# Splitting the second layer's mixing weights ahead in steps of three pieces

## The chip, the cores and the metric

The kernel runs on one core of one Trainium2 chip. The metric is the device time of one execution in microseconds (us); the time before is the median of three runs. Engines are named as in the profile: PE (TensorE matmuls), PEld (TensorE weight loads), DVE (VectorE), ACT (ScalarE), POOL (GpSimd), SP (SyncE, here the engine whose queue issues the DMAs).

## The reference

Two layers over 512 latent and 256 context tokens of width 1024. Each layer has a mixing part (one input projection `w_in`, then a gated MLP group A, a differential attention group B and a convolution group C, then one output projection `w_out`) and a gated feed-forward part of inner width 2816. Only the latent stream is returned. Cut to what matters here:

```python
for l in range(DEPTH):
    hl = modulate(rms_norm(x_lat, norm1_g[l]), sh1, sc1)
    pa, q, k, v, pc = project(hl, P, rope)            # hl @ w_in[l]
    o = blocked_diff_attn(q, k_all, v_all, lam)
    x_lat = x_lat + g1 * mixer_merge(pa, o, pc, P, lam_init)   # [ya, yb, yc] @ w_out[l]
    h2 = modulate(rms_norm(x_lat, norm2_g[l]), sh2, sc2)
    x_lat = x_lat + g2 * conv_ffn(h2, P)
def conv_ffn(h, P):
    gt = dwconv(h @ P["w_gate"], P["ffn_conv_w"], P["ffn_conv_b"])
    return (jax.nn.silu(gt) * (h @ P["w_val"])) @ P["w_down"]
```

The context tokens go through the same layer 0; in layer 1 they only give keys and values.

## The kernel before, in words

**Products.** Every FP32 product is made of three: each operand is split into a rounded part `hi` and a rest `lo = x - hi`, and PE adds hi·hi, hi·lo and lo·hi (`mm3`, L266 to L268). So each weight tile must be split before PE can use it: it is loaded as `raw` (L216, 512 KB for 128x1024), cast to `whi` on ACT (L224), and `wlo = raw - whi` follows on DVE or, for some tiles, on POOL (`sub_lo`, L110). `raw` has three buffers, `whi` and `wlo` two each, so the next cast waits until PE has left the tile before the last one.

**Feed-forward.** It runs in two halves of 11 inner tiles. A gate tile takes two weight tiles of `w_gv` (products `pp`), then `ft` (convolution, SiLU, product) and the split of its result into `gh` (ACT, L1028) and `gl`. After 11 gate tiles come four down steps (`w_down`, products `pd`), each over two output columns of `xT`; the last step of half 1, the tail, does the context and the latent tokens in two blocks.

**Splitting ahead.** Layer 1's mixing weights are split during layer 0's feed-forward by `split_ahead` (L237 to L252), a generator that is made at the end of half 0. For each of 56 pieces (40 of `w_in`, 16 of `w_out`, 128x512 each) it loads `araw` (L247), casts `ahi` (ACT, L248), subtracts in place (DVE, L110) and stores both parts to DRAM (L250, L251). Three buffers of each are there. Layer 1 then loads the finished parts as `wh` and `wl` (`wsplit_of`, L261) with no split. The code asks for three pieces after a gate tile of half 1 and for eight after a down step (`AHEAD`), at a priority lowered by 60 (`ALOW`). A scheduler orders each engine's instructions by priority and readiness; on the chip an engine runs them strictly in that order. The trace has the pieces between 598 and 789 us, that is from half 0's down steps on.

SP's queue is in order too: a load that has to wait until its buffer's store has landed holds every later load.

Of the kernel before, what the change touches and what calls it, by code (L numbers as in the profile page):

```python
# [53 lines left out]

WE = "dpdpdpdddppdpppppddp"


AHEAD = (3, 8)

AH = ((4, 1), (18, 1))  # L60
KH = ((6, 10, 27, 31, 35, 39), (17, 17, 25, 34, 35, 48))
CH = ((41, 3), (40, 5))
N1H, N1P = 5, 2
ALOW = 60

VEV = 2

# [13 lines left out]
def tile_backbone(  # L81
# [24 lines left out]
    def low(n):  # L106
        return tc.high_priority(offset=-n)
# [127 lines left out]
        return w_in[l, 2 * k2 * P:(2 * k2 + 2) * P, col:col + 512].rearrange("(a p) n -> p a n", p=P)  # L235

    def split_ahead(sp):  # L237
        todo = [(("in", col, k2), [w_cols(1, col, k2)[:, a] for a in range(2)])
                for col in (COL_K, COL_C, COL_A, COL_Q, COL_V) for k2 in range(KD // 2)]
        todo += [(("out", q, mp2), [w_out[1, q, mp2, :, i].rearrange("p k m -> p (k m)") for i in range(2)])  # L240
                 for mp2 in range(KD // 2) for q in range(2)]
        for key, srcs in todo:
            split[key] = dram.tile([P, 2, 2, 512], F32, name="_".join(map(str, key)))
            for a, src in enumerate(srcs):
                raw = sp.tile([P, 512], F32, tag="araw", name="araw", bufs=3)
                hi = sp.tile([P, 512], F32R, tag="ahi", name="ahi", bufs=3)
                nc.sync.dma_start(out=raw, in_=src)  # L247
                S.copy(hi, raw)  # L248
                sub_lo(raw, raw, hi)
                nc.sync.dma_start(out=split[key][:, 0, a], in_=hi.bitcast(F32))  # L250
                nc.sync.dma_start(out=split[key][:, 1, a], in_=raw)  # L251
                yield  # L252

    def wsplit_of(key, src, shape, eng, tags=("hi", "lo"), p=None, **kw):
        if key not in split:
# [18 lines left out]
    class Norm:  # L274
# [6 lines left out]
        def add(self, k, g):  # L281
            a, b, _ = g
            if g not in self.begun:
                self.begun.add(g)
                S.activation(self.ss[:, a:b], xT[:, k, a:b], AF.Square)
            else:
                sq = self.p.tile([P, 512], F32, tag="nsq", name="nsq", bufs=self.nb)
                S.activation(sq[:, :b - a], xT[:, k, a:b], AF.Square)
                V.tensor_add(self.ss[:, a:b], self.ss[:, a:b], sq[:, :b - a])

        def rstd(self, g, ps, tag, bufs):
            a, b, _ = g
# [29 lines left out]
    for l in range(DEPTH):  # L322
# [636 lines left out]
        with ExitStack() as ph:  # L959
# [22 lines left out]
            for half in range(2):  # L982
                gh = hp.tile([P, HJ, toks], F32R, tag="gh", name="gh", bufs=1)
                gl = hp.tile([P, HJ, toks], F32R, tag="gl", name="gl", bufs=1)
                for jj in range(HJ):
                    j = half * HJ + jj
                    pp = [[ps.tile([P, 512], F32, tag="acc", name="pp", bufs=8) for g in range(2)]
                          for s in range(nseg)]
                    w = [wsplit(w_gv[l, j, g], [KD, P], "dve") for g in range(2)]

                    def gv(g, seg):
                        a, b, s = seg
                        o = pp[s][g][:, a - SEG[s][0]:b - SEG[s][0]]
                        for k in range(KD):
                            mm3(o, w[g][0][:, k], w[g][1][:, k], hhi[:, k, a:b], hlo[:, k, a:b], k == 0, k == KD - 1)

                    if j == 0:
                        for seg in ngs:
                            if seg == g1:
                                for k in range(KD):  # L1000
                                    r = norm2.apply(l, 1, g1, k, hhi, hlo)
                                tab["since"].append(r.ins)
                                table(T_SILU)
                            for g in range(2):
                                gv(g, seg)
                                if seg == g0 and g == 1:
                                    norm2.rstd(g1, ps, "acc", 8)
                    else:
                        for g in range(2):
                            for seg in whole:  # L1010
                                gv(g, seg)
                    if j == 0 and not last:
                        start_dots(norm2.last)
                    t = sp.tile([P, TOK], F32, tag="ft", name="ft", bufs=FTB)
                    for s in range(nseg):
                        a, b = SEG[s]
                        gp = pp[s][0]
                        n = b - a
                        S.activation(t[:, a:b], gp[:, :n], AF.Identity, bias=fb[:, l, j:j + 1], scale=fw[:, l, j, 1:2])
                        V.scalar_tensor_tensor(out=t[:, a + 1:b], in0=gp[:, 0:n - 1], scalar=fw[:, l, j, 0:1],  # L1020
                                               in1=t[:, a + 1:b], op0=ALU.mult, op1=ALU.add)
                        V.scalar_tensor_tensor(out=t[:, a:b - 1], in0=gp[:, 1:n], scalar=fw[:, l, j, 2:3],  # L1022
                                               in1=t[:, a:b - 1], op0=ALU.mult, op1=ALU.add)
                    act(t[:, :toks], t[:, :toks], AF.Silu)
                    for s in range(nseg):
                        a, b = SEG[s]
                        V.tensor_mul(t[:, a:b], t[:, a:b], pp[s][1][:, :b - a])  # L1027
                    S.copy(gh[:, jj], t[:, :toks])  # L1028
                    sub_lo(gl[:, jj], t[:, :toks], gh[:, jj])
                    if not last and half:  # L1030
                        with low(ALOW):
                            for _ in zip(range(AHEAD[0]), ahead):
                                pass
                chunks = [(j0, min(4, HJ - j0)) for j0 in range(0, HJ, 4)]
                for mp2 in range(KD // 2):
                    tail = half == 1 and mp2 == KD // 2 - 1
                    ws = {}
                    for gi, gs in enumerate([[g] for g in ngs] if tail else [whole]):
                        pd = {g: [ps.tile([P, 512], F32, tag="acc", name="pd", bufs=8) for i in range(2)] for g in gs}
                        cs_ = chunks[::-1] if gi else chunks  # L1040
                        for ci, (j0, jn) in enumerate(cs_):
                            if not (gi and ci < 2):
                                src = w_down[l, mp2, :, half * HJ + j0:half * HJ + j0 + jn]
                                ws[j0] = wsplit(src, [jn, 256], "dve", p=wt if tail and not last else None)
                            wh, wl = ws[j0]
                            for jj in range(jn):
                                if gi and not last and (ci, jj) == (0, N1P):
                                    next_norm(ngs[0], ps, "acc", 8)
                                st_, sp_ = ci == 0 and jj == 0, ci == len(cs_) - 1 and jj == jn - 1
                                for g in gs:  # L1050
                                    a, b, s = g
                                    for i in range(2):
                                        ms = slice(i * P, (i + 1) * P)
                                        mm3(pd[g][i][:, :b - a], wh[:, jj, ms], wl[:, jj, ms],
                                            gh[:, j0 + jj, a:b], gl[:, j0 + jj, a:b], st_, sp_)
                        if not last and half:
                            with low(ALOW):
                                for _ in zip(range(AHEAD[1]), ahead):
                                    pass
                        for g in gs:  # L1060
                            a, b, s = g
                            for i in range(2):
                                m = 2 * mp2 + i
                                V.scalar_tensor_tensor(out=xT[:, m, a:b], in0=pd[g][i][:, :b - a],
                                                       scalar=modv[:, l, s, 5, m:m + 1],
                                                       in1=xT[:, m, a:b], op0=ALU.mult, op1=ALU.add)
                                if half == 1:
                                    if last:
                                        nc.sync.dma_start(out=out[:, m, a:b], in_=xT[:, m, a:b])
                                    else:  # L1070
                                        norm.add(m, g)
                        if tail and not last:
                            if gi == 0:
                                table(T_LNEXP)
                                hhi, hlo = [hb.tile([P, KD, TOK], F32R, tag=t, name=t) for t in ("hhi", "hlo")]
                if not last and half == 0:
                    dots.close()
                    cstack.close()
                    wt = pool(ph, "wt", "left")
                    ahead = split_ahead(wt)  # L1080
        pss_.close()
    hbs.close()
    nstack.close()
# [84 lines left out]
```

## Time and profile before

| what | us |
|---|---|
| median of three runs | 1620.43 (1617.92 to 1620.6) |
| profiled execution | 1616.07 |
| its span | 1614.0 |
| PE busy | 1570.6 (97%) |
| DVE busy | 1020.4 (63%) |
| ACT busy | 646.9 (40%) |
| POOL busy | 105.9 (7%) |

The profile comes from one execution, 4.4 us shorter than the median. PE is busy in nearly all of it, so time can be lost in two ways: PE idle, or PE at a lower granted clock (a column of its own, in shares of full speed). A wait is listed by engine, line, and what released it. Times at a row's start are us from the span's start; idle time before an instruction stands behind it in brackets.

### The profile page before, as it was taken

The page shows a single profiled execution, that of the slowest core. Times are in us where ns is not written, and L with a number is a line of the kernel's source. Part 1 is how long each engine was busy: PE and PEld are TensorE (multiplying, and loading weights), DVE is VectorE, ACT ScalarE, POOL GpSimd, SP SyncE. Part 2 cuts the span into 40 slices and gives each one's busy share as a digit, 9 for nine tenths or more (in the row PEclk, how much of TensorE's full clock was granted, in tenths as well). Part 3 has the DMA queues.
Part 4 walks back from the last instruction along what each step waited for, and adds up shares of the span by engine and source line. Part 5 has one row for each costly group of instructions (what it writes and reads, how often), then busy time and mean ns, then how long its engine had stood idle before and what let it go on. Part 6 is the DMA issues. An engine that isn't in the chain of part 4 may idle for free.

```text
span 1614.0 us, 21207 instructions
## 1 busy us (share of the span) xinstructions
PE 1570.6 (97%) x8186; PEld 1292.4 (80%) x8186; DVE 1020.4 (63%) x1722; ACT 646.9 (40%) x1122; POOL 105.9 (7%) x126
## 2 busy tenths in 40 slices
PE   6999998999999999999999999999999999999999
PEld 4875776778888887878888887887778788888888
DVE  4497878969999983345544244896976544334433
ACT  5431568753532322234433133254764333123321
POOL 1130125310000000000000000000220000000000
PEclk9999999999999999999999999999999999999999
DMA  7625110015255888988611235653022322332232
GB/s 282 212 76 180 56 64 15 14 51 185 85 190 194 285 279 265 289 284 298 207 66 50 60 127 186 205 170 105 27 80 78 104 92 88 95 104 92 92 105 92
DMA packets 83140, 222.93 MB, mean 138 GB/s; under 512 B 12256, under 2 KB 14560, under 8 KB 82912
## 3 DMA queue, kind: packets, MB, share of 16 engines
q1 hardware_dynamic: 83040, 221.59, 41.6%
q8 instruction: 64, 1.05, 0.3%
q14 instruction: 36, 0.29, 0.1%
HBM read 190.10 MB, written 31.46 MB: 137 GB/s over the span
## 4 chain that ended last, share of the span: by engine, by line
PE 77%; DMA 10%; DVE 6%; ACT 4%; issue 2%; SPq 0%; POOL 0%; POOLq 0%; DVEq 0%; ACTq 0%
PE pp L267 10%; PE pp L266 10%; PE pp L268 10%; PE acc L433 5%; PE acc L441 5%; PE acc L434 5%; PE pd L268 4%; PE pd L267 4%; PE pd L266 4%; DMA in<-araw 3%; DMA araw<-in_w_in_dram 3%; PE po L860 3%; PE wo L266 2%; DMA mraw<-in_w_modT_dram 2%; PE wo L267 2%; PE wo L268 2%
## 5 line engine op out<-in xcount | busy, mean ns | idle before, releaser
L268 PE MATMUL pp<-hhi,wlo 128*128 128x512 f32 (+1 forms) x1072 | 380.0, 355 | 4.4 <-DVE wlo L110 4.4
L266 PE MATMUL pp<-hhi,whi 128*128 128x512 f32 (+1 forms) x1072 | 380.6, 356 | 1.7 <-ACT whi L224 1.4
L267 PE MATMUL pp<-hlo,whi 128*128 128x512 f32 (+1 forms) x1072 | 381.4, 356 | 0.8 <-DVE hlo L306 0.8
L224 ACT CAST whi<-raw 128x1024 fp32r<-128x1024 f32 (+1 forms) x167 | 170.9, 1025 | 389.9 <-PE pp L267 203.0
L110 DVE TENSOR_TENSOR wlo<-raw,whi 128x1024 fp32r<-128x1024 f32 (+2 forms) x154 | 185.4, 1206 | 218.4 <-ACT whi L224 211.1
L268 PEld LDWEIGHTS pp<-hhi,wlo 128*128 128x128 f32 x1072 | 202.3, 189 | 36.1 <-DVE wlo L110 5.2
L266 PEld LDWEIGHTS pp<-hhi,whi 128*128 128x128 f32 x1072 | 202.0, 189 | 36.0 <-ACT whi L224 3.3
L267 PEld LDWEIGHTS pp<-hlo,whi 128*128 128x128 f32 x1072 | 202.0, 189 | 32.8 <-DVE hlo L306 1.5
L266 PE MATMUL pd<-gh,whi 128*128 128x512 f32 (+1 forms) x550 | 192.9, 351 | 2.5 <-ACT whi L224 2.5
L268 PE MATMUL pd<-gh,wlo 128*128 128x512 f32 (+1 forms) x550 | 193.6, 352 | 0.8 <-DVE wlo L110 0.8
L267 PE MATMUL pd<-gl,whi 128*128 128x512 f32 (+1 forms) x550 | 193.1, 351 | 0.0
L266 PEld LDWEIGHTS pd<-gh,whi 128*128 128x128 f32 x550 | 103.8, 189 | 18.0 <-ACT whi L224 2.9
L268 PEld LDWEIGHTS pd<-gh,wlo 128*128 128x128 f32 x550 | 104.1, 189 | 15.7 <-DVE wlo L110 1.0
L267 PEld LDWEIGHTS pd<-gl,whi 128*128 128x128 f32 x550 | 103.9, 189 | 15.1
L691 DVE SCALAR_TENSOR_TENSOR cacc<-cin,cw,cacc 128x783 f32<-128x783 f32 (+1 forms) x120 | 103.4, 916 | 3.4 <-ACT cacc L686 3.4
L110 DVE TENSOR_TENSOR araw<-araw,ahi 128x512 f32<-128x512 f32 x56 | 38.5, 691 | 93.3 <-ACT ahi L248 93.2
L1027 DVE TENSOR_TENSOR ft<-ft,pp 128x256 f32<-128x256 f32 (+1 forms) x66 | 39.1, 598 | 74.4 <-PE pp L268 66.7
L196 DVE CUSTOM_DVE_ANT_0 mraw<-mraw,csil,bmod 128x1024 f32<-128x1024 f32 x64 | 81.7, 1279 | 5.9 <-DMA mraw<-in_w_modT_dram 5.5
L248 ACT CAST ahi<-araw 128x512 fp32r<-128x512 f32 x56 | 34.7, 620 | 121.5 <-DMA araw<-in_w_in_dram 83.7
L433 PE MATMUL acc<-whi,hhi 128*128 128x512 f32 x192 | 77.8, 405 | 0.0
L434 PE MATMUL acc<-whi,hlo 128*128 128x512 f32 x192 | 76.9, 401 | 0.0
L101 ACT ACTIVATE ft<-ft 128x768 f32<-128x768 f32 (+1 forms) x44 | 32.6, 740 | 103.2 <-DVE ft L1022 103.2
(224 smaller groups left out, 2599.3 us busy)
## 6 DMA issues: line engine op xcount, KB each, us to landing
raw<-in_w_gv_dram SPq DMA_DIRECT2D x88, 512.0 KB, 3.3
mraw<-in_w_modT_dram SPq DMA_DIRECT2D x64, 512.0 KB, 4.3
raw<-in_w_down_dram SPq DMA_DIRECT2D x34, 512.0 KB, 3.6
wh<-in SPq DMA_DIRECT2D x24, 512.0 KB, 4.4
wl<-in SPq DMA_DIRECT2D x24, 512.0 KB, 4.5
raw<-in_w_in_dram SPq DMA_DIRECT2D x20, 512.0 KB, 4.1
araw<-in_w_in_dram SPq DMA_DIRECT2D x40, 256.0 KB, 3.6
in<-ahi SPq DMA_DIRECT2D x40, 256.0 KB, 4.7
```

The source lines that it names most:

```text
L110: (eng or V).tensor_sub(o, a, hi.bitcast(F32))
L196: r = V.tensor_tensor_reduce(out=junk, in0=w, in1=csil[:, s], scale=1.0, scalar=bmod[:, l, i, f:f + 1], op0=ALU.mult, op1=ALU.add, accum_o ...
L224: S.copy(hi, raw)
L266: T.matmul(o, lhi, rhi, start=start, stop=False)
L267: T.matmul(o, lhi, rlo, start=False, stop=False)
L268: T.matmul(o, llo, rhi, start=False, stop=stop)
L433: T.matmul(pt[t], hhi[hs], wh[:, a], start=k2 + a == 0, stop=False)
L434: T.matmul(pt[t], hlo[hs], wh[:, a], start=False, stop=False)
L441: T.matmul(pt[t], hhi[hs], wl[:, a], start=False, stop=k2 + 1 == KD // 2 and a == 1)
L691: V.scalar_tensor_tensor(out=cacc[:, c, :cn], in0=cin[:, c, j:j + cn], scalar=cw[:, l, c, j:j + 1], in1=cacc[:, c, :cn], op0=ALU.mult, op1 ...
L860: T.matmul(po, vt[:, kt, hs], at[:, c], start=c == 0, stop=c == nk - 1)
L1027: V.tensor_mul(t[:, a:b], t[:, a:b], pp[s][1][:, :b - a])
```

## The change

`split_ahead` is now sent an ACT instruction at each step. A step first splits the pieces that the step before loaded, with the casts ordered behind the instruction that was sent, and then loads up to three new pieces. It is sent the cast `gh` of each gate tile of half 1 and the last square of the norm (`norm.add`) of each down step, of the tail's first block alone in the last. Priority lowering and `AHEAD` are gone. The list has 44 pieces in place of 56: all 40 of `w_in`, and four of `w_out`. There are 15 steps, which load 44 and split 42; the last two pieces are loaded but not split. So one of eight `w_out` tiles of layer 1 comes split; the other seven are loaded raw and split in layer 1.

```diff
-        todo = [(("in", col, k2), [w_cols(1, col, k2)[:, a] for a in range(2)])
-                for col in (COL_K, COL_C, COL_A, COL_Q, COL_V) for k2 in range(KD // 2)]
-        todo += [(("out", q, mp2), [w_out[1, q, mp2, :, i].rearrange("p k m -> p (k m)") for i in range(2)])
-                 for mp2 in range(KD // 2) for q in range(2)]
-        for key, srcs in todo:
-            split[key] = dram.tile([P, 2, 2, 512], F32, name="_".join(map(str, key)))
-            for a, src in enumerate(srcs):
-                raw = sp.tile([P, 512], F32, tag="araw", name="araw", bufs=3)
+        todo = [(("in", col, k2), a, w_cols(1, col, k2)[:, a])
+                for col in (COL_K, COL_C, COL_A, COL_Q, COL_V) for k2 in range(KD // 2) for a in range(2)]
+        todo += [(("out", 0, mp2), i, w_out[1, 0, mp2, :, i].rearrange("p k m -> p (k m)"))
+                 for mp2 in range(2) for i in range(2)]
+
+        def load(src):
+            raw = sp.tile([P, 512], F32, tag="araw", name="araw", bufs=3)
+            nc.sync.dma_start(out=raw, in_=src)
+            return raw
+
+        ready = []
+        while todo or ready:
+            after = yield
+            for key, a, raw in ready:
+                if key not in split:
+                    split[key] = dram.tile([P, 2, 2, 512], F32, name="_".join(map(str, key)))
                 hi = sp.tile([P, 512], F32R, tag="ahi", name="ahi", bufs=3)
-                nc.sync.dma_start(out=raw, in_=src)
-                S.copy(hi, raw)
+                r = S.copy(hi, raw)
+                tc.add_manual_dep(r.ins, after.name, NOSYNC, reason="data of the step before")
                 sub_lo(raw, raw, hi)
                 nc.sync.dma_start(out=split[key][:, 0, a], in_=hi.bitcast(F32))
                 nc.sync.dma_start(out=split[key][:, 1, a], in_=raw)
-                yield
+            ready = [(key, a, load(src)) for key, a, src in todo[:3]]
+            todo = todo[3:]
+        while True:
+            yield
...
-                    S.copy(gh[:, jj], t[:, :toks])
+                    r = S.copy(gh[:, jj], t[:, :toks])
                     sub_lo(gl[:, jj], t[:, :toks], gh[:, jj])
                     if not last and half:
-                        with low(ALOW):
-                            for _ in zip(range(AHEAD[0]), ahead):
-                                pass
+                        ahead.send(r.ins)
...
-                        if not last and half:
-                            with low(ALOW):
-                                for _ in zip(range(AHEAD[1]), ahead):
-                                    pass
...
-                                        norm.add(m, g)
+                                        r = norm.add(m, g)
+                        if not last and half and not gi:
+                            ahead.send(r.ins)
...
                     ahead = split_ahead(wt)
+                    next(ahead)
```

Three places show what moves. **ACT**, at the first pieces. `ahi<-araw` is a piece's cast, `whi<-raw` that of a weight tile that PE waits for, `gh<-ft` the cast that ends a gate tile. Before, in half 0's down steps:

```order
L224 CAST whi<-raw 128x1024
L1028 CAST gh<-ft 128x768
L248 CAST ahi<-araw 128x512 x3
L224 CAST whi<-raw 128x768
L248 CAST ahi<-araw 128x512 x3
L224 CAST whi<-raw 128x1024
```

And now, in the gate tiles of half 1 (the line numbers have shifted):

```order
L220 CAST whi<-raw 128x1024
L1038 CAST gh<-ft 128x768
L253 CAST ahi<-araw 128x512 x3
L1029 ACTIVATE ft<-pp,fb,fw 128x256
L220 CAST whi<-raw 128x1024
L1029 ACTIVATE ft<-pp,fb,fw 128x512
L97 ACTIVATE ft<-ft 128x768
```

The casts have gone from half 0's down steps, where they stood between all weight casts, to one group of three in each gate tile of half 1, right behind `gh`.

**SP**, in the same two places; `in_1_...` is a split piece in DRAM. Before:

```order
L250 DMA in_1_6264<-ahi 128x512
L251 DMA in_1_6264<-araw 128x512
L247 DMA araw<-in_w_in_dram 128x512 x2
L216 DMA raw<-in_w_down_dram 128x768
L247 DMA araw<-in_w_in_dram 128x512
L250 DMA in_1_6264<-ahi 128x512
```

And now:

```order
L256 DMA in_1_6390<-ahi 128x512
L257 DMA in_1_6390<-araw 128x512
L243 DMA araw<-in_w_in_dram 128x512 x3
L212 DMA raw<-in_w_gv_dram 128x1024 x2
L256 DMA in_1_6390<-ahi 128x512
```

A group of three piece loads is now followed by the gate tile's two weight loads, and by stores only after these; before, piece loads and weight loads alternated in ones and twos.

**DVE**, in layer 1 at the end of the attention (`e` and `mx` belong to its softmax, `yBl` is the rest part of its result, `xT` the sum after the output projection). Before:

```order
L831 SCALAR_TENSOR_TENSOR e<-e,cc 128x768
L850 COPY ath<-pat 128x2x128
L875 SCALAR_TENSOR_TENSOR o<-o,gsub,osq 128x256
L110 TENSOR_TENSOR yBl<-o,yBh 128x256
L875 SCALAR_TENSOR_TENSOR o<-o,gsub,osq 128x256
```

And now:

```order
L841 SCALAR_TENSOR_TENSOR e<-e,cc 128x768
L106 TENSOR_TENSOR wlo<-raw,whi 128x1024
L106 TENSOR_TENSOR yBl<-o,yBh 128x256
L825 TENSOR_REDUCE mx<-pss 128x1
L860 COPY ath<-pat 128x2x128
L758 SCALAR_TENSOR_TENSOR xT<-wo,modv,xT 128x512
L838 RECIPROCAL cc<-sm 128x1
L839 SCALAR_TENSOR_TENSOR cc<-cc,nlam,sm 128x1
L841 SCALAR_TENSOR_TENSOR e<-e,cc 128x768
L885 SCALAR_TENSOR_TENSOR o<-o,gsub,osq 128x256
L860 COPY ath<-pat 128x2x128
L106 TENSOR_TENSOR yBl<-o,yBh 128x256
```

A weight tile's subtraction stands in the middle of the attention now, a second one right behind the last of these rows; ACT has the casts for both, and POOL has two further subtractions, one before and one within the attention.

## Rows read from the trace of the kernel before

**Rows 1.** Busy time by stretch: span, each engine, clock, DMA share, GB/s.

```profile
core 0: us, PE busy (x) PEld busy (x) DVE busy (x) ACT busy (x) POOL busy (x), PEclk, DMA share, GB/s
595.00:790.00 195.00, 187.19 (x1040) 161.76 (x1039) 93.13 (x133) 68.12 (x98) 0.00 (x0) 0.98 0.86 283
644.00:648.00 4.00, 4.00 (x16) 3.38 (x15) 3.85 (x7) 0.26 (x1) 0.00 (x0) 0.57 0.95 252
...
790.00:985.00 195.00, 195.00 (x1096) 169.22 (x1095) 79.61 (x119) 57.43 (x80) 1.46 (x1) 1.00 0.26 82
1125.00:1190.00 65.00, 62.40 (x335) 50.99 (x334) 59.78 (x111) 48.12 (x112) 18.16 (x33) 1.00 0.10 33
```

**Rows 2.** Waits from 595 to 790 us: total, times, longest.

```profile
ACT ahi L248 <- DMA araw<-in_w_in_dram: 83.7, 28, 8.7
...
PE pp L268 <- DVE wlo L110: 4.4, 4, 2.5
...
PE pd L266 <- ACT whi L224: 2.5, 1, 2.5
```

**Rows 3.** Timeline of PE at the longest of these waits.

```profile
639.08 0.40 PE L267 MATMUL pd<-gl,whi 128*128 128x512 f32 x1
639.31 0.39 PE L268 MATMUL pd<-gh,wlo 128*128 128x512 f32 x1
642.20 0.39 PE L266 MATMUL pd<-gh,whi 128*128 128x256 f32 x1 [2.50 <-ACT whi L224]
```

**Rows 4.** Timeline of ACT at the same place.

```profile
640.59 0.62 ACT L248 CAST ahi<-araw 128x512 fp32r<-128x512 f32 x1 [8.71 <-DMA araw<-in_w_in_dram]
641.11 1.04 ACT L224 CAST whi<-raw 128x1024 fp32r<-128x1024 f32 x1
```

**Rows 5.** Timeline of SP's queue at the same place.

```profile
633.77 6.53 SPq L247 DMA_DIRECT2D araw<-in_w_in_dram  x3
```

**Rows 6.** Timeline of ACT in a gate tile with no pieces beside it.

```profile
816.85 1.05 ACT L224 CAST whi<-raw 128x1024 fp32r<-128x1024 f32 x1 [3.74 <-PE pp L267]
...
825.29 1.05 ACT L224 CAST whi<-raw 128x1024 fp32r<-128x1024 f32 x1 [4.79 <-PE pp L267]
```

**Rows 7.** The tile `araw`: durations in ns, minimum, median, maximum; loads and stores landing.

```profile
L248 ACT CAST ahi<-araw x56: 605/620/622, 598.4 to 787.8; 128x512 fp32r<-128x512 f32 x56
L110 DVE TENSOR_TENSOR araw<-araw,ahi x56: 681/692/697, 599.0 to 788.4; 128x512 f32<-128x512 f32 x56
L247 SPq DMA_DIRECT2D araw<-in_w_in_dram x40: 328/333/1245, 595.7 to 728.3; - x40
...
DMA to landing us min/median/max: 2.5/3.9/6.7
```

**Rows 8.** A wait of PE in layer 1's output projection, 1190 to 1225 us.

```profile
PE wo L266 <- DMA wh<-out: 1.7, 2, 0.9
```

**Rows 9.** A wait of PE in layer 0's output projection, 345 to 400 us.

```profile
PE wo L266 <- DVE xT L748: 0.8, 1, 0.8
```

**Rows 10.** Splits of 128x1024 by line and form: count, busy us, mean ns, idle before.

```profile
L110 DVE TENSOR_TENSOR wlo<-raw,whi 128x1024 fp32r<-128x1024 f32 x137 | 169.4, 1238 | 173.3 <-ACT whi L224 166.2 <-issue 4.0
L224 ACT CAST whi<-raw 128x1024 fp32r<-128x1024 f32 x150 | 156.9, 1048 | 330.5 <-PE pp L267 203.0 <-PE pd L267 77.4 <-PE acc L434 20.3
```

**Rows 11.** Timeline of POOL and DVE around a POOL subtraction in layer 0.

```profile
226.28 2.70 POOL L110 TENSOR_TENSOR wlo<-raw,whi 128x1024 fp32r<-128x1024 f32 x1 [6.00 <-PE acc L441]
...
226.64 2.37 DVE L599 TENSOR_SCALAR rk<-rk 128x8 f32<-128x8 f32 x1
...
230.69 0.16 DVE L599 TENSOR_SCALAR rk<-rk 128x8 f32<-128x8 f32 x1
```

**Rows 12.** Timeline of DVE at the end of layer 1's attention.

```profile
1199.12 0.42 DVE L850 COPY ath<-pat 128x256 f32<-128x256 f32 x1 [1.63 <-PE pat L113]
...
1204.17 0.49 DVE L875 SCALAR_TENSOR_TENSOR o<-o,gsub,osq 128x256 f32<-128x256 f32 x1 [2.79 <-ACT osq L101]
```

**Rows 13.** Timeline of ACT in the tail of layer 0's feed-forward.

```profile
966.56 1.05 ACT L224 CAST whi<-raw 128x1024 fp32r<-128x1024 f32 x1 [0.24 <-PE pd L267]
```

More of the change, by code (lines that the diff above doesn't have):

```diff
@@ L55 @@
 WE = "dpdpdpdddppdpppppddp"
-AHEAD = (3, 8)
 AH = ((4, 1), (18, 1))
@@ L63 @@
 N1H, N1P = 5, 2
-ALOW = 60
 VEV = 2
@@ L284, in add @@
                 self.begun.add(g)
-                S.activation(self.ss[:, a:b], xT[:, k, a:b], AF.Square)
+                return S.activation(self.ss[:, a:b], xT[:, k, a:b], AF.Square)
             else:
                 sq = self.p.tile([P, 512], F32, tag="nsq", name="nsq", bufs=self.nb)
-                S.activation(sq[:, :b - a], xT[:, k, a:b], AF.Square)
+                r = S.activation(sq[:, :b - a], xT[:, k, a:b], AF.Square)
                 V.tensor_add(self.ss[:, a:b], self.ss[:, a:b], sq[:, :b - a])
+                return r
         def rstd(self, g, ps, tag, bufs):
```

## The prediction

> **What bounds the kernel now.** I read the busy time by stretch first, then the waits of the one stretch that stands out, then the timelines of PE, ACT and SP at its longest wait. PE bounds the kernel, and from 790 to 985 us, most of half 1 of layer 0's feed-forward, it is busy for 195.00 of 195.00 us. In the 195 us before, where the pieces are split ahead, it is busy for 187.19, and the DMA share is 0.86 against 0.26 [rows 1]. So 7.8 us of PE are idle there. The waits say on what: 4.4 us on `wlo` in four waits, 2.5 us on `whi` in one, the rest in small ones [rows 2].
>
> The timelines give the cause. PE starts a 512-column matmul every 0.23 us, then the start at 642.20 comes 2.89 us after the one before, because `whi` is late [rows 3]. That cast begins at 641.11, right behind a piece's cast at 640.59, for whose data ACT had stood idle for 8.71 us [rows 4]. The data were late because SP's three issues of pieces at 633.77 took 6.53 us [rows 5], where one issue takes 0.33 us at the median [rows 7]: an `araw` buffer has to be stored before it is filled again. ACT waits for piece data for 83.7 us in this stretch [rows 2], mostly while PE has work; where a weight cast is next in ACT's order, PE pays.
>
> PE pays twice. From 644 to 648 us, just after the 2.89 us, the granted clock is 0.57, about the lower level of 1.2 GHz [rows 1]; a second such stretch of 4 us follows the wait at 701 us. Each loses 4·(1 − 0.57) = 1.7 us.
>
> **The change part by part.** *Stalls that go.* Idle is 195.00 − 187.19 = 7.8 us, and the clock 2·1.7 = 3.4. Idle as printed understates a gap, since ends are modelled: the 2.50 us at 642.20 are 2.89 − 0.23 = 2.66 by starts [rows 3], that is 0.16 more; over the seven gaps of this kind 1.1. Together 12.3 us. They go if no weight cast stands behind a cast that waits for its data. A piece's cast stands behind `gh` of a gate tile and wants data whose load was issued in the tile before. Weight casts are 825.29 − 816.85 = 8.44 us apart in a gate tile [rows 6], so a tile is 16.9 us. From a cast to the data of the next piece in the same buffer it takes cast 0.62, subtraction 0.69, an issue 0.33, store 3.9, load 3.9 = 9.4 us by medians; with three casts in a row and two landings at 6.7 it is 16.3 [rows 7]. Both are under 16.9, and a down step is longer still (11·2·3 pairs of matmuls of 0.23 and 0.12 us, 23 us). So the data are there.
>
> *Work moved into half 1.* Three casts, 3·0.62 = 1.9 us, go behind `gh`; ACT is idle for 4.79 us before the next weight cast there [rows 6], so they are hidden. If that cover were gone, PE would wait up to 1.9 us in each of 11 tiles. Three subtractions, 2.1 us, join a DVE that is busy for 79.6 of 195 us [rows 1]. Taken at nought. Twelve pieces' work leaves this stretch for good, which also gives nought, as nothing but PE bounds it.
>
> *SP.* Each step queues six stores, then three loads, which wait for the stores' landing as now (6.5 us, [rows 5]). Behind them stand the next two gate weights. `raw` has three buffers, so a weight is asked for well over one 8.44 us half-tile ahead of its cast; the queue holds it up for less than that. Nought, up to 2 us.
>
> *The handover.* The tail's first block is half as wide, 11·2·3·0.12 = 7.9 us, less than the 9.4 of a median round trip, so its casts can wait 1.5 us or so for data, and the tail's last weight cast, which ACT runs at 966.56 [rows 13], is behind some of them. That cast comes about 1 us ahead of need. Between 0 and 2 us; I take 0.2, since the stores of the step before are long through when its loads go out.
>
> *Layer 1's output projection.* PE's two waits on loads of split `w_out` tiles, 1.7 us [rows 8], go: those tiles are not loaded split any more. Added are seven splits: seven casts of 1.05 us on ACT, five subtractions of 1.24 on DVE [rows 10] and two of about 2.7 on POOL [rows 11]. At most all is exposed: 7·1.05 + 5·1.24 + 2·2.7 = 18.9 us. At least none is, since layer 0's output projection splits all its tiles on the way with the same code and PE waits there for no `whi` or `wlo` worth naming, its longest wait is one of 0.8 us on `xT` [rows 9]. I go near that row, with two additions. One subtraction now stands within the attention, where DVE is busy for 59.78 of 65 us [rows 1]: counted whole, 1.2. One cast and one subtraction stand in the attention's end, 1.05 + 1.24 = 2.3; DVE has idle times of 1.63 and 2.79 us there [rows 12], so I count half, 1.1. Net 1.2 + 1.1 − 1.7 = +0.6; the ends that I keep are −1.7 and +4.5.
>
> *Sum.* −12.3 + 0.6 + 0.2 = −11.5 us: the profiled execution would go from 1616.07 to 1604.6. It lies 4.4 us under the median of the runs shown, so the median goes from 1620.43 to about 1609.
>
> **A rule against it.** In layer 0 a DVE instruction of 8 columns takes 2.37 us while POOL subtracts a weight tile, and 0.16 us a little later, with POOL free [rows 11]; DVE stood for nearly all of POOL's 2.70 us. One of the two new POOL subtractions falls within layer 1's attention, where DVE has 5.2 us to spare in 65 [rows 1]. So it can cost up to 2.7 us: rival two. The Trainium skill (SBUF — State Buffer, section "SBUF: two separate sides") has a rule for it: the port pair that DVE and GpSimd share is an exclusive lock, held for a whole instruction, and the loser fully blocks. By that rule the POOL subtraction always takes its 2.7 us from whichever DVE instruction needs the pair; the trace agrees at 226.64 us, though the instruction blocked there has one tensor input of 8 columns.
>
> **The rivals.** *One, the splits cost more than the stalls (slower).* Every one of the seven splits stands before PE in the attention or the output projection: +18.9. With the 12.3 and 1.7 gone that is +4.9, about 1625. For it speaks DVE at 92% in the attention and two buffers of each part; against it layer 0's projection [rows 9]. It decides once more than 17.2 us are exposed (14.0 plus 3.2). I give 6% to a good part being exposed, half of it past that point.
>
> *Two, POOL holds DVE in the attention.* +2.7 on the forecast: about 1612. For it [rows 11]; against it, that PE has other matmuls in the attention to go on with, and that DVE may have a chain with slack just then. 22%.
>
> *Three, the change doesn't do what it says.* Piece data still come late, because the stores wait on each other at SP, and ACT still stands in front of `whi`. With half the stalls left the gain is 5.3, about 1615; with all left the time is unchanged. For it, [rows 5]: the issue of loads waits for stores, and that stays. Against it, a whole tile between load and cast, 16.9 against 9.4 us. 8%, of which 3% with so much left that it can't be told from no change.
>
> **How the numbers follow.** My forecast has 64%, the rivals 6, 22 and 8. What a measurement of this kernel can tell from no change is about 0.2%, 3.2 us. Faster by more: 64 + 22 + 5 = 91%. Within: 3 + 3 = 6%. Slower by more: 3%. The range: the low end has nothing exposed in layer 1, −12.3 − 1.7 = −14.0, or 1606, less the 2.5 us by which the lowest run shown lies under the median: 1604. The high end takes in rival two and rival three with half the stalls left: 1615.
>
> **What would show it.** In the changed kernel's profile, the stretch from 595 to 790 us should have PE busy throughout at a clock of 1.00, with no wait of PE on `whi` or `wlo`. ACT's wait of `ahi` on `araw` should be near nothing in the gate tiles and at most a few us at the tail. PE's wait on `wh` loads at `w_out` should be gone, and small waits on `wlo` or on the softmax may stand in layer 1's attention. Wrong would be: a PE wait on `whi` in half 1 (rival three), or PE idle from 1125 to 1225 us by over 5 us more than now (rival one). A DVE instruction stretched beside the POOL subtraction in the attention, with PE waiting behind it, would be rival two.

## The result, and the profile of the changed kernel

The changed kernel takes 1602.73 us (median of four runs, 1602.73 to 1603.0), against 1619.37 us for the kernel before in the same series (four runs, 1617.92 to 1620.6). The ratio is 0.990 with a 95% interval of 0.9885 to 0.9915: 16.6 us faster. That is the direction that was forecast, but below the range of 1604 to 1615. The profiled executions stand at 1616.07 and 1602.73 us, 13.3 apart. How large the gain comes out depends on the series: in the three later ones, which the experiments come from, the kernel before had medians of 1615.34, 1618.63 and 1616.08 us.

The busy time by stretch of the changed kernel, columns as in [rows 1]; the last two stretches are the layer-1 attention and output projection, about 12 us earlier than before:

```profile
595.00:790.00 195.00, 195.00 (x1118) 170.55 (x1117) 74.86 (x103) 50.40 (x65) 0.00 (x0) 1.00 0.37 116
790.00:985.00 195.00, 195.00 (x1072) 168.09 (x1071) 98.32 (x152) 71.97 (x110) 1.46 (x1) 1.00 0.66 213
1113.00:1178.00 65.00, 61.83 (x335) 50.79 (x334) 60.61 (x113) 50.04 (x116) 22.29 (x32) 1.00 0.03 9
1178.00:1213.00 35.00, 33.28 (x157) 27.00 (x157) 21.53 (x34) 19.14 (x37) 2.98 (x3) 1.00 0.28 91
```

PE is busy throughout both halves of the 390 us, at full clock; before, the first of them had 187.19 of 195.00 [rows 1]. The DMA share of 0.86 there is now 0.37, and 0.66 in the second, to which the pieces have moved. In layer 1 the idle time of PE is 3.17 + 1.72 = 4.9 us in 100; before it was 2.60 [rows 1] and in the 35 us after that, by the same view of the kernel before, 2.59, together 5.2:

```profile
1190.00:1225.00 35.00, 32.41 (x153) 25.71 (x152) 15.23 (x29) 14.23 (x35) 3.06 (x4) 1.00 0.39 136
```

Waits in the changed kernel from 420 to 985 us (total, times, longest). These are the ones of piece casts on their data, and the only trace of `whi` on PE's side, a weight load's:

```profile
ACT ahi L253 <- DMA araw<-in_w_in_dram: 2.4, 1, 2.4
ACT ahi L253 <- DMA araw<-in_w_out_dram: 1.1, 1, 1.1
PEld pp L275 <- ACT whi L220: 0.8, 2, 0.4
```

Where ACT waited for `w_in` pieces 83.7 us in 28 waits [rows 2], it waits once; no matmul waits at all. (One weight cast, at 601.18, waits for 2.88 us, which the profile lists under the first three piece loads; no matmul waits behind it.) ACT's timeline shows how a gate tile now runs:

```profile
803.87 1.05 ACT L220 CAST whi<-raw 128x1024 fp32r<-128x1024 f32 x1 [3.74 <-PE pp L276]
804.88 0.84 ACT L1038 CAST gh<-ft 128x768 fp32r<-128x768 f32 x1
805.63 1.66 ACT L253 CAST ahi<-araw 128x512 fp32r<-128x512 f32 x3
807.19 0.56 ACT L1029 ACTIVATE ft<-pp,fb,fw 128x256 f32<-128x256 f32 x1
812.31 1.05 ACT L220 CAST whi<-raw 128x1024 fp32r<-128x1024 f32 x1 [4.57 <-PE pp L276]
```

Three casts in 1.66 us with no wait before them, and still 4.57 us of idle before the next weight cast, which PE releases. Compare [rows 4], where 8.71 us of waiting stood in front of a weight cast.

### The profile page after: what moved, and what is told of

Read it like the earlier page. It is cut to its first block, busy times and chain, and to the rows that moved or that the text cites. A ratio compares the mean times of both kernels' runs of the same rounds, so it can differ in the third digit from the quotient of the medians.

```text
span 1600.4 us, 21118 instructions
## 1 busy us (share of the span) xinstructions
PE 1565.2 (98%) x8186; PEld 1289.8 (81%) x8186; DVE 1016.0 (63%) x1713; ACT 643.3 (40%) x1115; POOL 113.3 (7%) x128
## 3 DMA queue, kind: packets, MB, share of 16 engines
q8 instruction: 64, 1.05, 0.3%
## 4 chain that ended last, share of the span: by engine, by line
PE 91%; DVE 4%; ACT 4%; issue 1%; DMA 0%; POOL 0%; POOLq 0%; DVEq 0%; SPq 0%; ACTq 0%
PE pp L276 13%; PE pp L275 13%; PE pp L277 13%; PE pd L277 6%; PE pd L276 6%; PE pd L275 6%; PE acc L443 5%; PE acc L451 5%; PE acc L444 5%; PE po L870 3%; PE wo L275 2%; PE wo L276 2%; PE wo L277 2%; PE mr L156 2%; ACT e L97 1%; PE accC L496 1%
## 5 line engine op out<-in xcount | busy, mean ns | idle before, releaser
L220 ACT CAST whi<-raw 128x1024 fp32r<-128x1024 f32 (+1 forms) x174 | 178.4, 1027 | 510.3 <-PE pp L276 248.4
L106 DVE TENSOR_TENSOR wlo<-raw,whi 128x1024 fp32r<-128x1024 f32 (+2 forms) x159 | 191.4, 1206 | 287.9 <-ACT whi L220 280.3
L97 ACT ACTIVATE e<-pss,mx 128x768 f32<-128x768 f32 (+1 forms) x80 | 65.1, 816 | 16.8 <-DVE mx L825 15.0
L825 DVE TENSOR_REDUCE mx<-pss 128x1 f32<-128x768 f32 (+1 forms) x80 | 67.3, 845 | 5.6 <-PE pss L823 4.6
```

Source lines behind the costliest of these rows:

```text
L97: r = S.activation(out, in_, func, **kw)
L106: (eng or V).tensor_sub(o, a, hi.bitcast(F32))
L825: V.tensor_reduce(out=mx, in_=pss[:, :nk * P], op=ALU.max, axis=AX.X, negate=True)
```

## The experiments

The main tool is one number for each profile: the PE time lost in the stretch of the pieces. It adds up, over the starts of neighbouring matmuls, what each distance exceeds the usual one of its two widths, so it holds idle and half-clock time alike. It is taken from 595 us to the end of the pieces (835 us; 850 for b2_twice, whose pieces run until 847). In the first profile of the kernel before it is 12.7 us. Beside it stands the longest time that a group of piece casts held ACT before a weight cast, from the end of the instruction before the group to the start of that cast (waits and casts together); for the kernels with the ordering line it is the casts' own time, since the weight cast behind them waits for PE and not for a piece.

| kernel | profiled us | lost in the stretch | longest hold of ACT |
|---|---|---|---|
| before, first profile | 1616.07 | 12.7 | 10.5 |
| before, second (again1) | 1621.17 | 17.4 | 11.3 |
| before, third (again2) | 1618.75 | 10.5 | 11.6 |
| list44 | 1612.96 | 10.6 | 10.7 |
| no_dep | 1613.77 | 10.9 | 11.3 |
| bufs4 | 1610.53 | 9.3 | 10.3 |
| lo128 | 1608.66 | 4.4 | 8.6 |
| two buffers (bufs2, bufs2b) | 1604.40, 1605.56 | 1.6, 3.2 | 8.9, 8.8 |
| b2_44 | 1607.00 | 3.3 | 8.6 |
| b2_twice | 1604.89 | 2.8 | 9.2 |
| changed kernel, same_step, out_dve | 1602.73, 1602.68, 1602.62 | 0, 0, 0 | 1.6 |

The profiled time less the loss is between 1601.2 and 1604.3 us in all of these executions but again2 (1608.2). So what sets these kernels apart is, to within some 3 us, what PE loses in this stretch.

**The list alone.** The 44 pieces in the kernel before:

```diff
-                 for mp2 in range(KD // 2) for q in range(2)]
+                 for mp2 in range(2) for q in range(1)]
```

> The kernel before, with only its list of pieces cut from 56 to the 44 of the change; the order of the pieces stays. My theory (the stalls come from piece casts that wait for their data among the weight casts, and their place in the order decides): PE still idles 5 to 9 us in the first 150 us of layer 0's second half of the feed-forward, less than now because there are 12 pieces fewer; layer 1 is as in the changed kernel, within 1 us; time 1614 to 1619. Rival (the 12 pieces less, that is less traffic and fewer casts, gave the gain): time 1603 to 1607, no PE wait on whi or wlo in that stretch.

It took 1612.72 us (10 runs, 1610.13 to 1617.83), the kernel before 1615.34 in that series (19 runs, 1610.77 to 1624.44); ratio 0.9976, 0.9961 to 0.9991. The stretch in its profile, and the waits there:

```profile
595.00:800.00 205.00, 199.19 (x1114) 172.20 (x1113) 94.27 (x133) 67.68 (x94) 0.00 (x0) 0.98 0.69 229
```

```profile
PE pd L266 <- ACT whi L224: 3.0, 2, 2.5
PE pd L268 <- DVE wlo L110: 1.2, 2, 0.8
PE pp L268 <- DVE wlo L110: 1.0, 2, 0.8
```

The time is below the 1614 to 1619 that I named, but the kernel before is lower by 4 us in this series than the time I had counted from. PE idles for 5.8 us in the stretch, inside the 5 to 9 I named: the stalls are still there. Layer 1 is 0.5 us shorter than before by the starts of DVE's instructions, as in the changed kernel. By the medians of this series the shorter list gains 2.6 us, a fifth of the 12.9 that the kernels with the ordering line gain in it. It is not the main cause.

**The ordering line alone taken away.** In the changed kernel:

```diff
                 r = S.copy(hi, raw)
-                tc.add_manual_dep(r.ins, after.name, NOSYNC, reason="data of the step before")
```

> The changed kernel without the one line that orders a piece's cast behind the instruction that the step is sent; the scheduler may then place the casts where it likes, and it puts them into half 0's down steps again. My theory (place decides): the stalls on whi and wlo come back, 8 to 15 us of lost PE time in that stretch, 1611 to 1619. Rival (the load one step ahead in the code gives the gain): 1602 to 1605 with PE busy throughout there.

1612.71 us (10 runs, 1610.4 to 1616.33), ratio to before 0.9983 (0.9969 to 0.9998): as slow as the list alone. PE and ACT at its longest wait:

```profile
639.77 0.40 PE L276 MATMUL pd<-gh,wlo 128*128 128x512 f32 x1
643.40 0.39 PE L274 MATMUL pd<-gh,whi 128*128 128x256 f32 x1 [3.23 <-ACT whi L220]
```

```profile
641.78 0.62 ACT L253 CAST ahi<-araw 128x512 fp32r<-128x512 f32 x1 [8.50 <-DMA araw<-in_w_in_dram]
642.30 1.04 ACT L220 CAST whi<-raw 128x1024 fp32r<-128x1024 f32 x1
```

It is the picture of [rows 3] and [rows 4] again, at the same place. Without the line the scheduler puts the casts into half 0's down steps, although the generator still loads one step ahead. So the line makes the gain of some 10 us by which the two kernels that keep it, below, were faster in the same series.

**Load and split in the same step**, with the ordering line kept:

```diff
-        ready = []
-        while todo or ready:
+        while todo:
             after = yield
-            for key, a, raw in ready:
+            for key, a, raw in [(key, a, load(src)) for key, a, src in todo[:3]]:
...
-            ready = [(key, a, load(src)) for key, a, src in todo[:3]]
```

> The changed kernel with load and split of a piece in the same step, the ordering behind the sent instruction kept. A load depends only on its buffer, so it is still issued as soon as the stores of the step before it are through, and the order of ACT and SP in the gate tiles is that of the changed kernel. My theory: 1601 to 1605, no ACT wait for piece data worth naming in the gate tiles. Rival (the step between load and split in the code is what makes the data early): ACT waits 4 to 8 us behind each gh, more than the 4.8 us of cover, PE loses 1 to 4 us in each of 11 tiles, 1614 to 1640.

1602.4 us (4 runs, 1600.56 to 1602.68), and PE busy for all of the stretch:

```profile
595.00:800.00 205.00, 205.00 (x1172) 179.17 (x1171) 81.26 (x111) 54.32 (x72) 0.00 (x0) 1.00 0.42 134
```

It also splits all 44 pieces, two more than the changed kernel. A group of loads on SP's queue, and the casts on ACT that use them:

```profile
729.62 2.77 SPq L243 DMA_DIRECT2D araw<-in_w_in_dram  x3
738.49 1.66 ACT L252 CAST ahi<-araw 128x512 fp32r<-128x512 f32 x3
```

So what the change calls its step ahead, written into the generator, is not needed: a load waits only for its buffer, and goes out 8.9 us before its casts by itself once these are held to their tile.

**POOL's subtractions on DVE**, for layer 1's output weights:

```diff
-            e = V if eng == "dve" else G if eng == "pool" or lo_n[0] % 2 else V
+            e = V if eng in ("dve", "out1") else G if eng == "pool" or lo_n[0] % 2 else V
...
-                w0 = wout_w(0, (0,), "pool")
+                w0 = wout_w(0, (0,), "out1" if last else "pool")
```

(and the same for the other call with "pool")

> The changed kernel with the two POOL subtractions of layer 1's output weights on DVE instead. Theory one (POOL's subtraction in the attention costs its 0.7 us wait of PE on POOL and nothing else): 0 to 1 us faster than the changed kernel, or the same. Theory two (the subtraction holds DVE, rival two of the prediction): 1.5 to 3 us faster. Theory three (DVE is the tighter engine in the attention): 1 to 2.5 us slower.

1602.39 us (4 runs, 1602.09 to 1602.7), within 0.4 us of the changed kernel, and equal to same_step in its own series: theory one, or no difference. POOL's place in the attention costs nothing that can be measured.

**The kernel before, twice more.**

> The kernel before, unchanged, for a second profiled execution and more times. My theory (the 4.4 us by which the first profiled execution lay under the median were stalls of the same kind, which differ from one execution to the next): the PE time lost in the stretch from 595 to 790 us differs from the first profile's 12.7 us by what the profiled time differs from 1616.07, within 1 us, and the rest of the program is the same within 0.5 us; the times spread over 2 to 4 us. Rival (the difference lies elsewhere, at the start or in layer 1): the stretch loses 12.7 again within 1 us while the time differs.

> The kernel before once more, for a third profiled execution. As for the second: by my theory its time differs from 1616.07 us by what the PE time lost from 595 to 790 us differs from 12.7 us, within 1 us; by the rival the stretch loses the same and the difference lies elsewhere.

The stretch from 595 to 800 us in the first, second and third profile:

```profile
595.00:800.00 205.00, 197.19 (x1094) 170.36 (x1093) 99.20 (x141) 72.06 (x104) 0.00 (x0) 0.98 0.83 275
```

```profile
595.00:800.00 205.00, 193.87 (x1074) 166.82 (x1073) 99.24 (x143) 72.21 (x104) 0.00 (x0) 0.98 0.85 274
```

```profile
595.00:800.00 205.00, 198.40 (x1109) 171.10 (x1109) 101.15 (x146) 73.99 (x106) 0.00 (x0) 0.99 0.83 276
```

The second bears my theory out: 17.4 us lost, 4.7 more, for a time 5.1 longer. Its ten runs had a median of 1620.46 us and spread over 5.4 (1616.88 to 1622.24), more than the 2 to 4 that I expected. The third does not: it lost 2.3 us less there and yet took 2.7 longer. Some 4 us of that lie in layer 1's output projection, where its waits are

```profile
PE wo L268 <- DMA wl<-out: 2.1, 1, 2.1
PE wo L266 <- DMA wh<-out: 1.8, 2, 1.0
```

against 1.7 in all in [rows 8], and a lower clock after them (0.96 from 1192 to 1235 us); some 1.2 us lie before 420 us, in a part that the change leaves alone. So executions differ both in the stalls of the pieces and in the loads of the split `w_out` tiles. The change removes both. Times agree: all runs of the kernel before lie between 1610.77 and 1624.63 us, all of the three kernels with the ordering line between 1600.56 and 1603.0.

**Two and four buffers** for the pieces in the kernel before (four for `araw` alone):

```diff
-                raw = sp.tile([P, 512], F32, tag="araw", name="araw", bufs=3)
-                hi = sp.tile([P, 512], F32R, tag="ahi", name="ahi", bufs=3)
+                raw = sp.tile([P, 512], F32, tag="araw", name="araw", bufs=2)
+                hi = sp.tile([P, 512], F32R, tag="ahi", name="ahi", bufs=2)
```

> The kernel before with two buffers of each piece tile in place of three. My theory (a piece's data are late because its buffer's store has to land first): fewer buffers, later data, longer SP waits, so PE loses 15 to 40 us in the stretch and the time is 1620 to 1645. Rival (the loss is the casts' and subtractions' own time on ACT and DVE): the loss stays at 11 to 14 us, 1614 to 1621.

> The kernel before with four buffers of araw in place of three. My theory (late data behind a store): the loads are issued earlier, PE loses 3 to 10 us in the stretch, 1608 to 1617. Rival (the order alone, whatever the buffers): 11 to 14 us as now, 1617 to 1621.

Two buffers give 1604.4 us (one run), four 1610.53 (5 runs, 1608.11 to 1614.55), the kernel before 1618.63 in that series. Four came out as my theory had it (9.3 us lost, 1608 to 1617). For two I was wrong by sign, under both theories, and with that the theory falls as a rule for the number of buffers. ACT waits longer in sum and PE does not pay (the stretch, the wait, and ACT at the longest hold, with two buffers):

```profile
595.00:800.00 205.00, 204.65 (x1167) 177.97 (x1166) 96.70 (x136) 69.92 (x98) 0.00 (x0) 1.00 0.74 246
```

```profile
ACT ahi L248 <- DMA araw<-in_w_in_dram: 99.3, 35, 6.5
```

```profile
646.94 0.62 ACT L248 CAST ahi<-araw 128x512 fp32r<-128x512 f32 x1 [6.44 <-DMA araw<-in_w_in_dram]
648.80 0.62 ACT L248 CAST ahi<-araw 128x512 fp32r<-128x512 f32 x1 [1.24 <-DMA araw<-in_w_in_dram]
649.33 0.83 ACT L224 CAST whi<-raw 128x768 fp32r<-128x768 f32 x1
```

The median landing of the pieces' transfers is 3.1 us with two buffers, 3.9 with three [rows 7], and 4.5 with four. The sum of ACT's waits is no measure of PE's loss. The longest single wait here is 6.5 us, against 8.7 [rows 2], but it is no sure measure either: b2_twice, below, has one of 7.8 us and loses 2.8, the third profile of the kernel before has none over 7.5 and loses 10.5.

**Traffic or the number of casts?** Two kernels, profiled once each, were to tell apart why two buffers help. With three buffers, less traffic (three quarters of each rest part are left out):

```diff
-                nc.sync.dma_start(out=split[key][:, 1, a], in_=raw)
+                nc.sync.dma_start(out=split[key][:, 1, a, :128], in_=raw[:, :128])
...
-            nc.sync.dma_start(out=flat.bitcast(F32), in_=split[key][:, x])
+            nc.sync.dma_start(out=flat.bitcast(F32), in_=split[key][:, 0])
```

> The kernel before, with three buffers, but of each piece's rest part only 128 of 512 columns are stored, and layer 1 reads the hi part in place of the rest: a quarter less traffic for the pieces. The order of ACT is nearly that of the kernel before, with slightly more casts between two weight casts. Theory one (a round of pieces through the DMA engines takes longer than the slack of a weight cast, and PE pays the excess): the rounds get shorter and PE loses 0 to 6 us in the stretch. Theory two (the number of casts in a group between two weight casts decides, 3 against 2): 10 to 18 us lost as in the kernel before.

With two buffers, more traffic:

```diff
                 nc.sync.dma_start(out=split[key][:, 1, a], in_=raw)
+                nc.sync.dma_start(out=spare[key][:, a], in_=raw)
```

> The kernel before with two buffers of each piece tile, and each rest part stored a second time to a spare place: a third more traffic for the pieces, with groups of at most two casts between weight casts. Theory one (length of a round): rounds grow, PE loses 3 to 12 us in the stretch. Theory two (casts in a group): 0 to 2 us lost, as with two buffers alone.

The stretch in the first and in the second:

```profile
595.00:800.00 205.00, 202.17 (x1142) 174.78 (x1141) 103.60 (x149) 76.04 (x108) 0.00 (x0) 1.00 0.69 225
```

```profile
595.00:800.00 205.00, 204.71 (x1169) 178.29 (x1169) 95.79 (x135) 67.88 (x95) 0.00 (x0) 1.00 0.84 291
```

The first speaks for theory one: groups of three casts, shorter rounds, 4.4 us lost. The second speaks against it: 291 GB/s, more than the kernel before moves, and only 2.8 us lost over all its pieces, between the 0 to 2 of theory two and the 3 to 12 of theory one. Neither holds alone. What fits both is the length of one hold of ACT: all kernels that held it for 10.3 us or more lost 9.3 to 17.4 us, all with 9.2 or less lost 4.4 or less. Fewer pieces in a batch, or less traffic for each, went with a shorter hold. This is read from the table and was not set by an experiment of its own, so why two buffers help stays open; and a long hold does not always reach PE, since the longest of the first profile, which ends at 654.65 us, had no matmul waiting behind it.

**Two buffers timed, and with the short list.** The second adds the list of 44 pieces to two buffers; both leave out the ordering line.

> The kernel with two buffers of each piece tile once more, to time it: 1602 to 1607, and if its stalls are really gone, with a spread of under 2 us; layer 1 still waits some 1.7 us for its split output weights. If the first look was a lucky execution, times scatter up to 1615.

> Two buffers of each piece tile and the list of 44 pieces in the kernel before, nothing else of the change. If the stretch's stalls and the waits for split output weights are all that the change removes, this reaches the changed kernel: 1601 to 1605, spread under 2 us. If the ordering behind the sent instruction gives something more, it stays at 1606 or above.

1605.35 us (4 runs, 1602.85 to 1607.29) and 1605.24 (4 runs, 1603.25 to 1607.0), the kernel before 1616.08. The shorter list adds nothing to two buffers, though it does remove the wait for split output weights: the median is the same, and the spreads, over 3.7 us each, are wider than the 2 us that I expected. The profiles show 3.2 and 3.3 us still lost to the pieces. So two buffers get most of the gain, and only the ordering line all of it: its kernels lie 2.5 to 3 us lower, though they were timed in other series (10.7 and 10.8 us below the kernel before here, 12.9 and more there).

## Why the prediction missed, point by point

- **The stalls that go: right.** I counted 12.3 us; by starts it was 12.7 in that execution, and nothing is left. The chain from late piece data over ACT's order to a late `whi` was the right one at 642 us: with the casts back in half 0's down steps (no_dep) it came back at the same place. But the prediction read one stall of two. The second long one, at 704 us, came over DVE's order, in the kernel before:

```profile
700.01 1.05 ACT L224 CAST whi<-raw 128x1024 fp32r<-128x1024 f32 x1
700.14 0.69 DVE L110 TENSOR_TENSOR araw<-araw,ahi 128x512 f32<-128x512 f32 x1 [1.91 <-ACT ahi L248]
700.75 2.19 DVE L1064 SCALAR_TENSOR_TENSOR xT<-pd,modv,xT 128x256 f32<-128x256 f32 x4
702.85 1.22 DVE L110 TENSOR_TENSOR wlo<-raw,whi 128x1024 fp32r<-128x1024 f32 x1
704.12 0.39 PE L268 MATMUL pp<-hhi,wlo 128*128 128x256 f32 x1 [2.46 <-DVE wlo L110]
```

`whi` was there at 701.06. DVE stood waiting for a late piece, then did that piece's subtraction and four sums into `xT`, whose products PE had finished by 691.7, and only then the `wlo` that PE needed. The ordering line moves this subtraction too, since it follows the piece's cast.

- **Why the data are there in time: right in its result, wrong in its reason.** There are 16.9 us from one group of casts to the next, but a load does not go out a whole tile ahead of its cast: here it is issued 8.8 us before. That is enough, and it comes from the ordering line and free buffers; the step in the generator is not needed (same_step). My account of SP, that data are late because a buffer must be stored first, suggested that more buffers help; two helped more than four.

```profile
796.80 2.83 SPq L243 DMA_DIRECT2D araw<-in_w_in_dram  x3
805.63 1.66 ACT L253 CAST ahi<-araw 128x512 fp32r<-128x512 f32 x3
```

- **Casts and subtractions in half 1: right.** No matmul waits there, and 4.57 us of ACT's cover of 4.79 [rows 6] are left.
- **The handover: right.** ACT waits there for 2.43 and 1.05 us, in place of the 1.5 that I named, and the tail's last weight cast follows without idle, as [rows 13] had next to none; PE does not wait in the tail.

```profile
952.64 0.62 ACT L253 CAST ahi<-araw 128x512 fp32r<-128x512 f32 x1 [2.43 <-DMA araw<-in_w_in_dram]
954.32 0.62 ACT L253 CAST ahi<-araw 128x512 fp32r<-128x512 f32 x1 [1.05 <-DMA araw<-in_w_out_dram]
```

- **Layer 1's output weights: right in kind, off by 0.9.** I took +0.6; PE's idle time went from 5.2 to 4.9 us, −0.3. The 1.7 us on `wh` loads [rows 8] are gone, and new waits of 1.4 us more on `e`, 0.7 on POOL and 0.3 more on `osq` have come, 2.4 together, as much as the 2.3 that I had added. What I did not foresee is that a wait of 1.0 us of `pss`, for which the profile names no cause, went too. The cast and subtraction in the attention's end, which I had counted half, were covered wholly: PE does not wait there on `whi` or `wlo`. The waits of the kernel before, 1125 to 1190 us, and of the changed kernel, 1113 to 1213 us:

```profile
PE pss L812 <- issue: 1.0, 1, 1.0
PE pat L113 <- DVE e L831: 0.4, 1, 0.4
```

```profile
PE pat L109 <- DVE e L841: 1.8, 3, 0.8
PE pss L822 <- POOL wlo L106: 0.7, 1, 0.7
PE pr L882 <- POOL osq L875: 0.7, 1, 0.7
```

- **Rival two, POOL holding DVE: not so, though the hold is seen.** POOL's subtraction ran from 1122.08 for 2.38 us. In it DVE finished a reduction, a reciprocal and a copy in their usual times; one instruction was held. In the changed kernel, and the same form in the kernel before:

```profile
1122.08 2.38 POOL L106 TENSOR_TENSOR wlo<-raw,whi 128x1024 fp32r<-128x1024 f32 x1 [0.98 <-ACT whi L220]
1123.73 0.74 DVE L839 SCALAR_TENSOR_TENSOR cc<-cc,nlam,sm 128x1 f32<-128x1 f32 x1
```

```profile
1190.57 0.22 DVE L829 SCALAR_TENSOR_TENSOR cc<-cc,nlam,sm 128x1 f32<-128x1 f32 x1
```

It ends with POOL's at about 1124.46. So the price was 0.5 us of DVE, not 2.7. The rule of the Trainium skill (SBUF — State Buffer, "SBUF: two separate sides") is borne out by this row. The prediction's reading of it, that POOL always takes its full 2.7 us from DVE, is not: what it costs depends on when DVE next has an instruction that needs the shared pair.

- **The sum's transfer to the median: here it failed.** Against its own execution the sum gave −11.5; measured was −13.3, and the parts above account for 13.0 (12.7 and 0.3). Had only the sum been set right, to −13.3, the forecast would have been 1607, inside the range. But I carried over the 4.4 us by which the profiled execution lay under the median, as if it were a fixed offset between the two, and gave 1609. The later profiles of the kernel before show what such a gap is made of: one was 5.1 us longer, 4.7 of it in the stretch of the pieces, the other 2.7 longer with some 4 us more around the `w_out` loads. These are, but for 1.2 us before 420 us, the waits that the change removes, and the profiled execution of the changed kernel is at its median, 1602.73. Nor is the 4.4 a mark of the kernel: it was counted from three runs, and the medians of 1615.34, 1618.63 and 1616.08 us in the later series lie 0.7 us below to 2.6 above that same profile. The mean of the three profiles of the kernel before, 1618.7, is 15.9 us above it. Without the 4.4 us the forecast would have been 1604.6. The low end of the range had the same fault: it was counted from the median too, and 1604 was reached only by adding the scatter of the old kernel; the same −14.0 taken from the profiled execution gives 1602.1.

What stays open is the rest of the difference between 13.3 and 16.6 us. Three profiles of the kernel before show its kind, waits timed by DMA, but not its size in the four timed runs, which have no profile; and in the series of 1615.34 us two kernels with the ordering line gained 12.9 and not 16.6. The part before 420 us also varied by up to 1.2 us, in a part that both kernels share; from 240 to 300 us its granted clock was 0.94, 0.89 and 0.91 in the three profiles. No experiment looked into that.

## What to carry to other kernels

When an engine runs in order, put work that waits for a transfer behind an instruction that comes late enough for its data, rather than giving it a low priority: without the ordering line the scheduler put the casts, low in priority (before) or not (no_dep), in front of weight casts that PE needed. Follow that order on every engine that the late work runs on, here DVE as well as ACT. Read the longest single hold in front of an urgent instruction, not the sum of waits. And if runs scatter while the stalls are timed by DMA, a gap between the profiled execution and the median may be part of the stalls: a change that removes them can take the gap with it.

## What the hardware showed that was not expected

With fewer piece buffers in flight the pieces' transfers landed sooner (median 3.1, 3.9 and 4.5 us for two, three and four), and two buffers lost 1.6 to 3.2 us of PE time where the kernel before, with three, lost 10.5 to 17.4. A kernel that moved 291 GB/s in the stretch lost less (2.8 us) than one at 275 (12.7), so the rate alone doesn't tell of stalls. PE waits up to 0.8 us each, with 2.8 us in all, left the granted clock at 1.00 over the stretch (lo128), where a single stop of 2.9 us between starts was followed by 4 us at 0.57 [rows 1, 3].
